# Split weights that begin 16 bytes lower with each turn through their three slots, and normalised x 32 bytes lower

## The chip, the core and the metric

The kernel runs on one core of one Trainium2 chip. The metric is the device time of one execution in microseconds. The core has five engines that run side by side: TensorE (PE in the profile, with PEld for its weight loads), VectorE (DVE), ScalarE (ACT), GpSimd (POOL) and SyncE (SP), which here issues DMAs. SBUF is the on-chip memory of 128 partitions; PSUM is where matmuls put their sums.

## The reference

One layer of a hybrid decoder on 512 tokens and 16 meta tokens (528 columns, called L), width 2048, all in float32:

```python
n = _rmsnorm(h, g_mix)                      # h: (528, 2048)
q, k, v, gb, gc, u = split(n @ w_in)        # six groups of 1024 columns
q, k = _rmsnorm(q, g_q), _rmsnorm(k, g_k)   # per head, 8 heads x 128
o_attn = stick_breaking_attention(q, k, v)  # strictly causal, cumulative log weights
o_conv = gb * causal_dwconv3(gc * u)
h = h + concat(_rmsnorm(o_attn), _rmsnorm(o_conv)) @ w_out
n2 = _rmsnorm(h, g_ffn)
h = h + (silu(n2 @ w_gate) * (n2 @ w_up)) @ w_down   # d_ff = 5632
```

## The kernel before

All activations are held transposed, channels on partitions and tokens along the row. To keep float32 accuracy with the fast float32r matmul, every weight and every activation is split into a high and a low part, and each 128x128 piece of a product is three matmuls: high weights by high activations, and the two mixed products. Every matmul has a weight load of its own, 128 columns of 4 bytes in each partition. The activations are the moving operand, 256, 258, 272 or 512 columns of 4 bytes.

**The split weights.** A piece is eight 128x128 tiles of raw weights, loaded by DMA into `sw_in`. `split_quad` (L197) splits it into `sw_split`: ACT copies the high part (L204), DVE subtracts to get the low part (L207). `sw_split` holds three slots of 8192 bytes in each partition, 4096 of high and 4096 of low parts. Pieces take the slots in turn, so a turn is three pieces, and the splits run two pieces ahead of PE (`S_AHEAD`, L153). The first ten pieces, which take part in the start of the program, lie in the same space as six halves of a slot, by another rule (L202). `prepare` (L236) says which piece is next, and `next_w` (L301) hands PE the oldest one. The order of all instructions follows from the program's own order, priorities and a tile scheduler.

**The normalised x.** Sixteen tiles `n_tiles` (L380) hold the high and the low part of x scaled by the norm's gain, each part a row of 528 columns. The tile has 160 bytes of free room ahead of what is used, and the low part stands 2304 bytes (nine times 256) behind the high part. A tile is 4608 bytes, eighteen times 256, so all sixteen begin at the same place modulo 256.

**Where they begin.** `pad_h` and `pad_n` are unused tiles that shift what is allocated around them. In the program as built, `sw_split` begins at byte 202624 of each partition, 128 modulo 256, and tile `n0` is used from byte 104256, 64 modulo 256. Slots, tiles within a slot, and the two parts are multiples of 512 bytes apart, so every weight load of split weights begins at 128 modulo 256. A matmul on `n` begins at 64 plus four bytes for each column that it skips.

**Who reads the normalised x.** `product_steps` (L327) makes the products of the heads: for each head k and v (each 256 and 272 columns, lines L337 and L339, tiles pk and pv) and q (512 columns from token 16 on, so 64 bytes further, tile pq). For each piece it runs 24 matmuls of one column part and then 24 of the other. Between them stand the small matmuls of the attention of the head before. After the eight heads come the first conv channels (`cu_product` L721, pc and pu, 258 columns, 56 bytes in; pb, 512 columns). Then `pair_product` (L861) makes the rest of the convolution in seven products for each pair of tiles, by a Strassen-like scheme, with `block_product` (L832, lines L848, L851, L852, 24 matmuls each). Four of the seven read `n` directly (`raw_block` L789, `last_block` L796), three read mixed sums of x kept in tiles `mixed`. `conv_pair` reads 258 columns, `gate_pair` 256 columns 8 bytes further. `last_block` begins 1032 bytes further on, which is 8 modulo 256.

**What does not read it.** The output projection reads tiles oa and oc, the FFN reads tiles f (and later ring and first); both take their weights from `sw_split`. The tiles f, ring and first are used from 240 modulo 256, the tiles mixed step by 8 bytes from tile to tile, and oa and oc are at 128.

Of the kernel before, what the change touches and what calls it, by code (L numbers as in the profile page):

```python
# [9 lines left out]
F32 = mybir.dt.float32  # L10
F32R = mybir.dt.float32r
# [4 lines left out]
P = 128  # L16
# [17 lines left out]
def hybrid_layer(ctx: ExitStack, tc: tile.TileContext, xT, w_in, w_out, w_gu, w_down, vecs, out):  # L34
# [12 lines left out]
    def open_pool(name, bufs=1, **kw):  # L47
        return tc.alloc_tile_pool(name=name, bufs=bufs, reuse_waits="tile", **kw)
# [3 lines left out]
    sw = open_pool("sw", side="right")  # L52
    npool = open_pool("npool", side="right")
# [50 lines left out]
    acc_h = hpool.tile([P, SEQ], F32, name="acc_h")  # L104
    hpool.tile([P, 24], F32, name="pad_h")
    sw_in = sw.tile([P, 6 * 8 * P], F32, name="sw_in")
    sw_split = sw.tile([P, 6 * 8 * P], F32R, name="sw_split")

    def w_place(t, n, i):
        return t[:, i * n * P : (i + 1) * n * P]  # L110
# [41 lines left out]
    quads, sums, split_w, used, wide, raws = {}, {}, [], [0], {}, []  # L152
    S_AHEAD = 2  # L153
# [42 lines left out]

    def split_quad(src, n, half=None, later=False):  # L197
        if half is None:
            at = (len(split_w) + 1) % (S_AHEAD + 1) * 16 * P
            hi, lo = (sw_split[:, at + i * n * P : at + (i + 1) * n * P] for i in range(2))  # L200
        else:
            at = half * 8 * P  # L202
            hi, lo = (sw_split[:, at + i * 4 * P : at + (i * 4 + n) * P] for i in range(2))
        sc.copy(hi, src)  # L204

        def low():
            latest[0] = ve.tensor_tensor(lo, src, hi.bitcast(F32), ALU.subtract)  # L207

        if not later:
            low()  # L210
        split_w.append((hi, lo))
        return low
# [23 lines left out]
    def prepare():  # L236
        kind, i, s = pieces[len(split_w)]
        with tc.high_priority():
            if kind == "first":
                at = len(split_w)  # L240
                split_quad(raws[at], s - i, at % 6)
                if at + 1 == n_first:
                    for i in (2, 3):
                        tc.keep_in_program_order(load_wide(0, i))
                return
            if kind == "wide":
                split_quad(wide[i, s], 8)
                load_wide(i, s + 4)
                return
# [4 lines left out]
            if s == 0:  # L254
                if i - 1 in (0, CONV):
                    low = split_quad(b["11"], n, later=True)

                    def rest():
                        low()
                        if i - 1 == CONV:  # L260
                            add_quads(i, "t1", b["11"], b["12"])
                        load_next(i, "11")

                    put_off.append(rest)
                    if i - 1 != CONV:
                        add_quads(i, "t1", b["11"], b["12"])
                    return
# [111 lines left out]
    H = L // 2  # L379
    n_tiles = [npool.tile([P, 2, L + 48], F32R, name=f"n{k}")[:, :, 40:] for k in range(KT)]  # L380
    n_parts = [[t[:, part] for part in range(2)] for t in n_tiles]
    npool.tile([P, 52], F32, name="pad_n")
    n_hl = []
    accs = [rpool.tile([P, L], F32, name=f"acc_x{i}") for i in range(2)]

# [103 lines left out]
    for t, row in zip(hosts, ((("kh", 384), ("kl", 384), ("sh", L), ("sl", L)), (("qh", SEQ), ("ql", SEQ), ("bh", 288), ("bl", 288)))):  # L489
        at = 0  # L490
# [659 lines left out]
    at = [(c, k) for c, n in enumerate(CHUNKS) for k in range(n)]  # L1150
# [199 lines left out]
```

## Time and profile before

| | |
|---|---|
| Runs | median of three 2032.04 us, from 2031.81 to 2034.05 |
| Profiled execution | 2031.66 us, of which 2029.9 us lie between the first and the last instruction |
| PE busy | 2021.6 us, clock granted in full throughout |
| DVE, ACT, POOL busy | 1725.7, 1080.3, 338.7 us |
| PE matmuls on `n` | 448.64 us of busy time, all before 600 us |
| Start to 30 us | first ten pieces, k and q of head 0 |
| 30 to 336 us | v of head 0, heads 1 to 7 |
| 336 to 387 us | first conv channels |
| 387 to about 600 us | conv in pairs |
| 600 to 2030 us | output projection, FFN |

A matmul row's duration in the profile runs from its issue to the end of its pipeline, longer than its share of PE: starts of successive matmuls are closer together than their durations are long. The spacing of starts is what a matmul costs in a stream, and is read from the timeline, from the first start of a stretch to the first start behind it, divided by the matmuls between. "x2" in a timeline row is two matmuls merged into one row.

### The profile page before, as it was taken

How to read it: one execution, taken by the hardware profiler on the slowest of the kernel's cores; microseconds unless marked ns; L12 is line 12 of the kernel's file. 1: busy time of each engine (PE TensorE's matmuls, PEld its weight loads, DVE VectorE, ACT ScalarE, POOL GpSimd, SP SyncE). 2: the span in 40 equal slices, each digit the busy share in tenths (PEclk: the TensorE clock that was granted, in tenths of full speed). 3: DMA queues.
4: the chain of work that ended last, by engine and by line, in shares of the span. 5: the costliest groups of instructions: out<-in, count | busy, mean ns of one | idle time of the engine just before them, and what ended most of it. 6: DMA issues, size and time to landing. Idle time of an engine off the chain costs nothing.

```text
span 2029.9 us, 39684 instructions
## 1 busy us (share of the span) xinstructions
PE 2021.6 (100%) x16158; PEld 1962.7 (97%) x16158; DVE 1725.7 (85%) x2196; ACT 1080.3 (53%) x1556; POOL 338.7 (17%) x507
## 2 busy tenths in 40 slices
PE   9999999999999999999999999999999999999999
PEld 8999999999998889999999999999999999999999
DVE  7877777698887778999998998998988978888888
ACT  7776666444454445555555555555555554444443
POOL 0111111200014440111110110110110243131211
PEclk9999999999999999999999999999999999999999
DMA  6343343823355555557555555555555999797864
GB/s 221 100 141 125 118 143 128 286 99 114 98 204 174 169 160 193 165 153 192 158 165 157 156 167 156 155 168 157 155 167 157 284 342 352 171 315 196 221 150 91
DMA packets 156231, 356.30 MB, mean 176 GB/s; under 512 B 13648, under 2 KB 67920, under 8 KB 155280
## 3 DMA queue, kind: packets, MB, share of 16 engines
q1 hardware_dynamic: 72352, 216.76, 33.4%
q0 software_dynamic: 83696, 136.99, 25.3%
q8 instruction: 127, 2.08, 0.4%
q14 instruction: 56, 0.46, 0.1%
HBM read 275.78 MB, written 77.92 MB: 174 GB/s over the span
## 4 chain that ended last, share of the span: by engine, by line
PE 50%; DVE 0%; issue 0%
PE x L848 10%; PE x L851 10%; PE x L852 10%; PE z L851 5%; PE z L848 5%; PE z L852 5%; PE y L851 2%; PE y L848 2%; PE y L852 2%; DVE d L1248 0%; DVE d L1250 0%
## 5 line engine op out<-in xcount | busy, mean ns | idle before, releaser
L204 ACT CAST sw_split<-sw_in 128x1024 fp32r<-128x1024 f32 (+2 forms) x668 | 662.9, 994 | 706.7 <-PE x L851 177.7
L207 DVE TENSOR_TENSOR sw_split<-sw_in,sw_split 128x1024 fp32r<-128x1024 f32 (+2 forms) x668 | 776.9, 1164 | 140.1 <-ACT sw_split L204 135.0
L848 PE MATMUL x<-f,sw_split 128*128 128x256 f32 x1408 | 387.6, 275 | 1.0 <-ACT sides L873 0.8
L852 PE MATMUL x<-f,sw_split 128*128 128x256 f32 x1408 | 387.4, 275 | 0.9 <-DVE sw_split L207 0.9
L851 PE MATMUL x<-f,sw_split 128*128 128x256 f32 x1408 | 387.3, 275 | 0.0
L848 PEld LDWEIGHTS x<-f,sw_split 128*128 128x128 f32 x1408 | 264.3, 188 | 1.7 <-ACT sides L873 1.2
L852 PEld LDWEIGHTS x<-f,sw_split 128*128 128x128 f32 x1408 | 264.3, 188 | 1.1 <-DVE sw_split L207 1.1
L851 PEld LDWEIGHTS x<-f,sw_split 128*128 128x128 f32 x1408 | 264.3, 188 | 0.0
L1159 POOL DMA_DIRECT2D fd<-s x147 | 103.9, 920 | 708.7 <-DVE s L350 633.2
L217 DVE TENSOR_TENSOR sw_in<-sw_in 128x1024 f32<-128x1024 f32 (+1 forms) x164 | 187.8, 1146 | 6.9 <-DMA sw_in<-w_in 1.5
L848 PE MATMUL z<-f,sw_split 128*128 128x256 f32 x704 | 193.6, 275 | 0.0
L851 PE MATMUL z<-f,sw_split 128*128 128x256 f32 x704 | 193.6, 275 | 0.0
L852 PE MATMUL z<-f,sw_split 128*128 128x256 f32 x704 | 193.6, 275 | 0.0
L848 PE MATMUL x<-ring,sw_split 128*128 128x256 f32 x608 | 167.2, 275 | 0.0
L851 PE MATMUL x<-ring,sw_split 128*128 128x256 f32 x608 | 167.2, 275 | 0.0
L852 PE MATMUL x<-ring,sw_split 128*128 128x256 f32 x608 | 167.2, 275 | 0.0
L852 PEld LDWEIGHTS z<-f,sw_split 128*128 128x128 f32 x704 | 132.2, 188 | 0.0
L851 PEld LDWEIGHTS z<-f,sw_split 128*128 128x128 f32 x704 | 132.2, 188 | 0.0
L848 PEld LDWEIGHTS z<-f,sw_split 128*128 128x128 f32 x704 | 132.1, 188 | 0.0
L848 PEld LDWEIGHTS x<-ring,sw_split 128*128 128x128 f32 x608 | 114.1, 188 | 0.0
L852 PEld LDWEIGHTS x<-ring,sw_split 128*128 128x128 f32 x608 | 114.1, 188 | 0.0
L851 PEld LDWEIGHTS x<-ring,sw_split 128*128 128x128 f32 x608 | 114.1, 188 | 0.0
(691 smaller groups left out, 5283.3 us busy)
## 6 DMA issues: line engine op xcount, KB each, us to landing
sw_in<-w_gu SPq DMA_DIRECT2D x176, 512.0 KB, 4.1
sw_in<-w_in SPq DMA_DIRECT2D x92, 512.0 KB, 3.4
fd<-s POOLq DMA_DIRECT2D x147, 256.0 KB, 5.2
sw_in<-w_down SPq DMA_DIRECT2D x96, 384.0 KB, 4.3
ring<-fd POOLq DMA_DIRECT2D x42, 768.0 KB, 17.5
sw_in<-w_out SPq DMA_DIRECT2D x32, 512.0 KB, 3.5
out_T<-d POOLq DMA_DIRECT2D x54, 256.0 KB, 4.8
mix_dram<-st_x POOLq DMA_DIRECT2D x16, 516.0 KB, 4.1
```

The source lines that it names most:

```text
L204: sc.copy(hi, src)
L207: latest[0] = ve.tensor_tensor(lo, src, hi.bitcast(F32), ALU.subtract)
L217: return ve.tensor_tensor(sums[name], a, b, ALU.add)
L848: opening = pe.matmul(p, hi[:, kk], ah, start=start and j == k == 0, stop=False, skip_group_check=skip)
L851: pe.matmul(p, hi[:, kk], al, start=False, stop=False, skip_group_check=skip)
L852: pe.matmul(p, lo[:, kk], ah, start=False, stop=k == n - 1, skip_group_check=skip)
L1159: gp.dma_start(fd[c][s][:, :, k], t[:, :, i])
```

## The change

Two things are edited, and one follows from them. `sw_split` gets 64 more columns (256 bytes). During the heads a piece no longer begins at its slot's beginning but up to 240 bytes behind it: `turn` counts the turns through the three slots, and the piece begins `max(18 - turn, 0) * 4` columns, so 16 bytes for each turn still to come, behind the slot's beginning. The first piece that goes this way is in turn 3 (240 bytes), the last piece of head 7 in turn 18 (0 bytes). All later pieces lie at the slot's beginning as before. The unused tile `pad_n` is dropped.

```diff
-    sw_split = sw.tile([P, 6 * 8 * P], F32R, name="sw_split")
+    sw_split = sw.tile([P, 6 * 8 * P + 64], F32R, name="sw_split")
...
     def split_quad(src, n, half=None, later=False):
         if half is None:
-            at = (len(split_w) + 1) % (S_AHEAD + 1) * 16 * P
+            turn, at = divmod(len(split_w) + 1, S_AHEAD + 1)
+            at = at * 16 * P + max(18 - turn, 0) * 4
             hi, lo = (sw_split[:, at + i * n * P : at + (i + 1) * n * P] for i in range(2))
         else:
             at = half * 8 * P
...
     n_tiles = [npool.tile([P, 2, L + 48], F32R, name=f"n{k}")[:, :, 40:] for k in range(KT)]
     n_parts = [[t[:, part] for part in range(2)] for t in n_tiles]
-    npool.tile([P, 52], F32, name="pad_n")
```

The pools on that side are allocated downwards. `sw_split` now begins 256 bytes lower (still 128 modulo 256), and with `pad_n` gone (224 bytes with its rounding) the tiles `n` begin 32 bytes lower, at 32 modulo 256. Where the operands begin, modulo 256, and the weights' begin minus that of x, here called the relation:

| stream | x before | weights before | relation before | x after | weights after | relation after |
|---|---|---|---|---|---|---|
| k, v (256, 272 columns) | 64 | 128 | 64 | 32 | 112, then each 16 lower, to 128 | every multiple of 16 |
| q (512) | 128 | 128 | 0 | 96 | the same | sweeps too |
| pc, pu, raw blocks (258) | 120 | 128 | 8 | 88 | 128 | 40 |
| last block (258) | 128 | 128 | 0 | 96 | 128 | 32 |
| raw blocks of gates (256) | 128 | 128 | 0 | 96 | 128 | 32 |
| last block of gates (256) | 136 | 128 | 248 | 104 | 128 | 24 |
| pb0, pb1 (512) | 128 | 128 | 0 | 96 | 128 | 32 |
| f, ring, first (256, FFN) | 240 | 128 | 144 | 240 | 128 | 144 |

Over the heads, k and v get 72 matmuls of each column count at each multiple of 32, and 24 at each odd multiple of 16. The relation stays the same through a piece and its 48 matmuls.

The order of the instructions is the same on every engine, and so are the waits, except two: the high part of the piece with index 10 waits for one more subtraction on DVE, and the low part of the piece with index 11 for a later matmul (PE's count 133 instead of 118), since the shifted pieces reach 224 to 240 bytes into the neighbouring half that one of the first ten pieces used.

## The prediction

> **What bounds the kernel now.** I read the page's first and fourth parts, then the stages, then single starts on the timeline.
>
> ```profile
> span 2029.9 us, 39684 instructions
> PE 2021.6 (100%) x16158; PEld 1962.7 (97%) x16158; DVE 1725.7 (85%) x2196; ACT 1080.3 (53%) x1556; POOL 338.7 (17%) x507
> PE 50%; DVE 0%; issue 0%
> PE warm L84 <- DVE one L80: 1.1, 1, 1.1
> ```
>
> PE is busy for the whole span, the chain that ended last names nothing else of weight, and PE's longest wait is 1.1 us. So the time is the sum of the spacings of matmuls, and only what changes a spacing counts. The change moves no instruction; it moves the places in SBUF that matmuls on `n` and their weight loads read. Busy time of PE on tile n, by stage:
>
> ```profile
> 0.00:30.00 30.00, 23.65 (x142) 1.00 0.85 304
> 30.00:336.00 306.00, 260.81 (x1774) 1.00 0.38 121
> 336.00:387.00 51.00, 45.58 (x293) 1.00 0.71 240
> 387.00:520.00 133.00, 74.53 (x606) 1.00 0.41 131
> 520.00:600.00 80.00, 44.07 (x360) 1.00 0.49 164
> ```
>
> Some 450 us are exposed; behind 600 us nothing reads n, and begins modulo 256 stay. Does the place matter at all? First starts, from the timeline (start, duration, engine, line):
>
> ```profile
> 1499.74 0.28 PE L852 MATMUL x<-f,sw_split 128*128 128x256 f32 x1
> 1503.03 0.28 PE L851 MATMUL z<-f,sw_split 128*128 128x256 f32 x1
> ...
> 178.91 0.28 PE L337 MATMUL pk<-n,sw_split 128*128 128x256 f32 x1
> 181.74 0.29 PE L337 MATMUL pk<-n,sw_split 128*128 128x272 f32 x1
> 184.70 0.39 PE L337 MATMUL pq<-n,sw_split 128*128 128x512 f32 x1
> 186.74 0.39 PE L337 MATMUL pq<-n,sw_split 128*128 128x512 f32 x1
> 188.08 0.40 PE L337 MATMUL pq<-n,sw_split 128*128 128x512 f32 x1
> 190.16 0.39 PE L337 MATMUL pq<-n,sw_split 128*128 128x512 f32 x1
> ...
> 440.82 0.28 PE L848 MATMUL x<-n,sw_split 128*128 128x258 f32 x1
> 443.71 0.28 PE L848 MATMUL y<-n,sw_split 128*128 128x258 f32 x1
> 446.57 0.28 PE L848 MATMUL x<-n,sw_split 128*128 128x258 f32 x1
> ...
> 460.81 0.28 PE L848 MATMUL x<-n,sw_split 128*128 128x256 f32 x1
> 463.85 0.28 PE L848 MATMUL y<-n,sw_split 128*128 128x256 f32 x1
> 466.72 0.28 PE L848 MATMUL x<-n,sw_split 128*128 128x256 f32 x1
> ```
>
> It does. With 256 columns and the same work:
> - f (relation 144): 3.29 us for 29 matmuls, 113.4 ns each
> - k (relation 64): 181.74 - 178.91 = 2.83 us for 24, 117.9 ns
> - gate block (relation 0): 466.72 - 463.85 = 2.87 us for 24, 119.6 ns
> - gate's last block (relation 248): 463.85 - 460.81 = 3.04 us for 24, 126.7 ns
>
> So a matmul costs up to 13.3 ns more than at the best place. My reading, which these rows suggest but don't prove, is that the stream of x and the load of the next matmul's weights, which run together, sometimes want the same part of SBUF, and the relation sets how often. Part of it is a matter of state: the 512-column q at relation 0 runs at 2.04 us for 9, 226.7 ns, and after the attention's small matmuls at 2.08 us for 9, 231.1 ns. Relation 64 knows two states too, here in head 1:
>
> ```profile
> 44.29 0.39 PE L339 MATMUL pk<-n,sw_split 128*128 128x256 f32 x2
> 45.31 0.39 PE L339 MATMUL pk<-n,sw_split 128*128 128x256 f32 x2
> ```
>
> 1.02 us for 9 is 113.3 ns, the best spacing, at a place that mostly gives 117.9.
>
> The Trainium skill, TensorE: Matmul & The Clock Gate, Part 2, step 1, says that PE has two independent SBUF read ports, one for the moving operand and one for weight loads, so that loading the next weights takes nothing from the running matmul. By that rule places do nothing and the sum is zero. The rows above disagree, 113.4 against 126.7 ns, and the measurement decides.
>
> **What is over the floor today.** From 256 columns at 113.4 to 512 at 226.7 ns a column costs 0.443 ns, so I take as floors (estimates) 114.3 ns for 258 columns and 120.5 for 272. Above them, by count of matmuls:
> - k and v, 256 columns: 4.5 ns x 720 = 3.2 us
> - k and v, 272 columns: (184.70 - 181.74) / 24 = 123.3 ns, so 2.8 x 720 = 2.0 us
> - q: between 0 and 4.4, about 2.2 x 336 = 0.7 us
> - 258 columns at relation 8: 2.86 / 24 = 119.2 ns, so 4.9 x 696 = 3.4 us
> - 258 columns at relation 0: 2.89 / 24 = 120.4 ns, so 6.1 x 168 = 1.0 us
> - gates: 6.2 x 216 + 13.3 x 72 = 2.3 us
> - pb: at the floor by the 226.7 of q, 96 matmuls
>
> Together 12.6 us is the most that better places could give back.
>
> **The change, part by part.** In the heads the relation sweeps all 16 multiples of 16, so the new price is a mean over them. No row shows such a sweep with one relation held for 48 matmuls. Bounds are 0 (f) and 13.3 ns (gate's last block). The nearest rows are the mixed tiles, which step through all places in steps of 8 bytes, three blocks of 24 each:
>
> ```profile
> 432.18 0.28 PE L848 MATMUL z<-mixed,sw_split 128*128 128x258 f32 x1
> 440.82 0.28 PE L848 MATMUL x<-n,sw_split 128*128 128x258 f32 x1
> ...
> 452.31 0.28 PE L848 MATMUL z<-mixed,sw_split 128*128 128x256 f32 x1
> 460.81 0.28 PE L848 MATMUL x<-n,sw_split 128*128 128x256 f32 x1
> ```
>
> 8.50 us for 72 is 118.1 ns, 4.7 over the floor with 256 columns; 8.64 for 72 is 120.0, 5.7 over with 258. The relations held at multiples of 16 (144, 64, 0) cost 0, 4.5 and 6.2, mean 3.6. Between 3.6 and 4.7 I take 4.2 ns for every stream of the heads:
> - 256 columns: (4.2 - 4.5) x 720 = -0.2 us
> - 272 columns: (4.2 - 2.8) x 720 = +1.0 us
> - q: (4.2 - 2.2) x 336 = +0.7 us
>
> After the heads each stream gets one new relation between 24 and 40, of which no row has a held price. Bounds are again 0 and 13.3. For 258 columns I take 5.5, between the held 4.9 and 6.1 and near the mixed 5.7: 0.6 x 696 - 0.6 x 168 = +0.3 us. For the gates the mixed 4.7: -1.5 x 216 - 8.6 x 72 = -0.9 us. For pb 4.2: +0.4 us.
>
> The start of the program (142 matmuls on n before 30 us, which wait for x) I cost at nothing, within 0.5 us either way.
>
> The splits, with 44 pieces at shifted places, I cost at nothing. Their engines have room in the heads, and pieces are two ahead:
>
> ```profile
> 30.00:336.00 306.00, 305.37 (x2099) 285.29 (x2098) 234.24 (x401) 217.18 (x361) 41.49 (x112) 1.00 0.38 121
> L204 ACT CAST sw_split<-sw_in 128x1024 fp32r<-128x1024 f32 (+2 forms) x668 | 662.9, 994 | 706.7 <-PE x L851 177.7
> 33.38 2.36 DVE L207 TENSOR_TENSOR sw_split<-sw_in,sw_split 128x1024 fp32r<-128x1024 f32 x2 [1.04 <-ACT sw_split L204]
> 24.08 1.06 ACT L204 CAST sw_split<-sw_in 128x1024 fp32r<-128x1024 f32 x1 [0.61 <-DMA sw_in<-w_in]
> 30.52 0.28 PE L337 MATMUL pv<-n,sw_split 128*128 128x256 f32 x1
> 36.31 0.28 PE L337 MATMUL pv<-n,sw_split 128*128 128x256 f32 x1
> ```
>
> The columns behind the length are busy time of PE, PEld, DVE, ACT, POOL: DVE idles 72 us of 306, ACT 89. Were the 44 copies of 994 ns twice as long, their 44 us would still fit, though DVE's subtractions wait behind them. Of the two new waits, that of piece 10's high part has the copy at 24.08 us, 5.4 us ahead of the first reader at 30.52; queued behind it on ACT is the read of pk, and a subtraction more is 1.2 us at most. That of piece 11's low part holds DVE, where the subtractions of pieces 11 and 12 stand at 33.38 us. The matmuls it must now await lie before pv's first at 30.52, so the wait ends 2.9 us ahead, and the piece is read from 36.31. No cost; were that cover gone, PE would be late by what passes 36.31. Further down, FFN and output projection keep their relations: zero.
>
> Sum: -0.2 + 1.0 + 0.7 + 0.3 - 0.9 + 0.4 = +1.3 us. The profiled execution took 2031.66 us, 0.4 under the median of the runs, and gives 2033.0.
>
> **Rivals.** *Slower, by bad places.* Relation 248 cost 13.3 ns. If 5 of the 16 relations of the sweep cost that and the others 4.2, the heads' mean is 7.0, and the heads give 2.5 x 720 + 4.2 x 720 + 4.8 x 336 = 6.4 us: 2038. It is over 0.2% from a mean of 5.8 ns on. For it speaks that 0 and 248 are both dear, so a dear stretch may be wide; against it that 248 came with x off the 16-byte grid, and every begin stays on it in the heads.
>
> *Faster, by locking.* The best spacing appears at relation 144 always and at 64 at times. If half of the heads' relations lie at the floor, mean 1.8, the heads give -2.7 x 720 - 1.0 x 720 - 0.4 x 336 = -2.8 us; if the relations 24 to 40 are at half of today's price as well, 6.7 / 2 = 3.4 us more: 2025.5. For it speaks head 1; against it that the mixed tiles, which pass every place, never come near the floor on average.
>
> *Nothing at all.* Were the places without effect, as the rule above has it, 2031.7. The rows leave it little.
>
> **How the numbers follow.** A measurement of this kernel tells about 0.2%, 4.1 us, from no change. The averaging case 0.55, bad places 0.27, locking 0.15, nothing 0.03; of the averaging case and its neighbours a few hundredths cross the bound either way. The time is the averaging case's 2033.0. Prices of 2 to 7 ns in the heads move it by about -4 to +5 us, and the relations after the heads at 2 or 8 ns by -4 to +3; the range 2027.5 to 2039 holds both rivals but their ends, the averaging case alone 2029 to 2036. Faster 0.15, the same 0.57, slower 0.28.
>
> **What would show it.** In the changed profile, k and v of different heads must differ in length, where now all heads are alike, with the spacing of 256 columns between 113 and 127 ns head by head; the gates' last block must fall from 126.7; f must stay at 113.4. The waits of PE must stay near 1 us in all. I am wrong if the heads' spacings hardly move (then the relation is not what matters), if the mean over the sweep lies below 2 or above 7 ns, or if PE waits for splits.

## The result, and the profile after

| | before | after |
|---|---|---|
| Median of 18 runs each | 2031.65 us | 2034.65 us |
| Ratio | | 1.0014, interval 1.0007 to 1.0020 |
| Profiled execution, span | 2029.9 us | 2032.7 us |
| PE busy | 2021.6 us | 2024.4 us |

The change costs about 3 us, 0.14%, inside the bound of 0.2%. The span and PE's busy time both grow by 2.8 us. First the page of the changed kernel (span, busy time by engine) and its longest PE wait:

```profile
span 2032.7 us, 39684 instructions
PE 2024.4 (100%) x16158; PEld 1964.2 (97%) x16158; DVE 1725.6 (85%) x2196; ACT 1078.9 (53%) x1556; POOL 338.9 (17%) x507
PE 50%; DVE 0%; issue 0%
PE warm L84 <- DVE one L80: 1.1, 1, 1.1
```

No wait was added: the longest is the 1.1 us of before. So the loss is in the matmuls. Busy time of PE on tile n in the changed kernel, by the same stages as in the prediction:

```profile
0.00:30.00 30.00, 23.54 (x142) 1.00 0.84 304
30.00:336.00 306.00, 260.90 (x1751) 1.00 0.38 121
336.00:387.00 51.00, 45.60 (x300) 1.00 0.65 219
387.00:520.00 133.00, 77.75 (x620) 1.00 0.44 136
520.00:600.00 80.00, 43.68 (x360) 1.00 0.50 168
sum 600.00, PE 451.47; mean PE 90.29
```

The sum is 451.47 us against 448.64, so the matmuls on n account for 2.83 us, all of the loss. Between 30 and 336 us the same busy time holds 1751 matmuls instead of 1774: the heads are slower, and some twenty matmuls slide into later stages (one that crosses a border counts in both). First starts in the changed kernel's timeline (start, duration, engine, line; lines between the edits are one further down):

```profile
129.24 0.28 PE L338 MATMUL pk<-n,sw_split 128*128 128x256 f32 x1
132.12 0.29 PE L338 MATMUL pk<-n,sw_split 128*128 128x272 f32 x1
...
179.73 0.28 PE L338 MATMUL pk<-n,sw_split 128*128 128x256 f32 x1
182.53 0.28 PE L338 MATMUL pk<-n,sw_split 128*128 128x272 f32 x1
...
74.96 0.29 PE L338 MATMUL pv<-n,sw_split 128*128 128x272 f32 x1
78.00 0.28 PE L338 MATMUL pv<-n,sw_split 128*128 128x256 f32 x1
...
285.65 0.29 PE L338 MATMUL pv<-n,sw_split 128*128 128x272 f32 x1
288.62 0.28 PE L338 MATMUL pv<-n,sw_split 128*128 128x256 f32 x1
...
269.66 0.40 PE L338 MATMUL pq<-n,sw_split 128*128 128x512 f32 x1
271.75 0.39 PE L338 MATMUL pq<-n,sw_split 128*128 128x512 f32 x1
...
464.16 0.28 PE L848 MATMUL x<-n,sw_split 128*128 128x256 f32 x1
467.04 0.28 PE L848 MATMUL y<-n,sw_split 128*128 128x256 f32 x1
469.89 0.28 PE L848 MATMUL x<-n,sw_split 128*128 128x256 f32 x1
...
1501.75 0.28 PE L851 MATMUL x<-f,sw_split 128*128 128x256 f32 x1
1503.11 0.28 PE L851 MATMUL x<-f,sw_split 128*128 128x256 f32 x1
```

Heads now differ, as the prediction asked. Blocks of 24:
- k of head 3 at relation 0: 2.88 / 24 = 120.0 ns; k of head 4 at relation 224: 2.80 / 24 = 116.7 (before: 117.7 to 117.9 in all heads, but for two blocks of head 1 at 113.3 to 113.5)
- 272 columns, v of head 1 at relation 48: 126.7 ns; v of head 6 at relation 144: 123.8 (before: 123.3)
- q of head 6 at relation 80: 2.09 / 9 = 232.2 ns (before: 226.7 to 231.1)
- the gates' last block: 120.0 (before 126.7); the gate block behind it 118.8 (before 119.6)
- f: 1.36 / 12 = 113.3, unchanged

Worked out from all starts of both traces, the 2.8 us split up like this (sums of spacings by product):

| part | change, us |
|---|---|
| heads 1 to 7: k, q, v | +0.85, +0.84, +1.04 |
| head 0, start of the program included | -0.2 |
| pc, pu | +0.2 |
| pb0, pb1 | +0.6 |
| conv in pairs | -0.6 |
| output projection | +0.2 |
| attention, FFN | -0.1 |

### The profile page after: what moved, and what is told of

It is laid out like the page before. It is cut to its first block, busy times and chain, and to the rows that moved or that the text cites. A ratio compares the mean times of both kernels' runs of the same rounds, so it can differ in the third digit from the quotient of the medians.

```text
span 2032.7 us, 39684 instructions
## 1 busy us (share of the span) xinstructions
PE 2024.4 (100%) x16158; PEld 1964.2 (97%) x16158; DVE 1725.6 (85%) x2196; ACT 1078.9 (53%) x1556; POOL 338.9 (17%) x507
## 4 chain that ended last, share of the span: by engine, by line
PE 50%; DVE 0%; issue 0%
PE x L848 10%; PE x L851 10%; PE x L852 10%; PE z L848 5%; PE z L851 5%; PE z L852 5%; PE y L848 2%; PE y L851 2%; PE y L852 2%; DVE d L1248 0%; DVE d L1250 0%
```

## The experiments

Three theories stood. A: the relation (weights' begin minus x's begin, modulo 256) sets the spacing. B: x's own begin does. C: neither, but the strides of the tiles or what ran just before. The diffs of the single parts stand against the kernel before, those further down against the changed kernel; those of the tables show their loops alone.

### A table of spacings

The layer is left out. Blocks of 24 matmuls (eight tiles, three matmuls each, each with its own weight load, as in the heads) run back to back for 16 begins of x times 16 begins of weights, with 256 and then with 272 columns.

```diff
+    for n in (256, 272):
+        for x_at in range(0, 256, 16):
+            for w_at in range(0, 256, 16):
+                block(n, x_at, w_at, 1152, 576)
```

> The layer is left out; only matmuls are timed, in groups of 24 that stream x past split weights with the strides of the heads. x begins at each of the 16 multiples of 16 modulo 256, the weights too, 256 groups with 256 columns and 256 with 272. Theory A (the relation, weights' begin minus x's begin, sets the spacing): the table is constant along its diagonals, 113.4 ns with 256 columns at relation 144, 118 at 64, 120 at 0. Theory B (the begin of x alone sets it): constant for each begin of x, lowest at 240. Theory C (neither; the state in which a stream falls, and the strides between the two parts of x): no pattern along rows, columns or diagonals, and a spread of a few ns.

Four neighbouring block starts with x at 32 (weights at 80, 96, 112 and the next), then two blocks with x at 48 (weights at 112 and 160), from the timeline:

```profile
124.52 0.28 PE L68 MATMUL bank<-both 128*128 128x256 f32 x1
127.34 0.28 PE L68 MATMUL bank<-both 128*128 128x256 f32 x1
130.07 0.28 PE L68 MATMUL bank<-both 128*128 128x256 f32 x1
132.92 0.28 PE L68 MATMUL bank<-both 128*128 128x256 f32 x1
...
175.53 0.28 PE L68 MATMUL bank<-both 128*128 128x256 f32 x1
178.25 0.29 PE L68 MATMUL bank<-both 128*128 128x256 f32 x1
...
183.94 0.28 PE L68 MATMUL bank<-both 128*128 128x256 f32 x1
186.67 0.28 PE L68 MATMUL bank<-both 128*128 128x256 f32 x1
```

With x at 32: 2.82 us at relation 48, 2.73 at relation 64, 2.85 at relation 80. Of these three only relation 64 is at the low spacing (113.3 ns in the middle of the block). With x at 48 relation 64 gives 2.72 us and relation 112 gives 2.73: both are low. The table is nearly constant along its diagonals, but there are two such patterns, one for x at 0 modulo 32 and one for x at 16 modulo 32. So theory A holds with a second condition. Exceptions remain: at relation 112 with x at 16 modulo 32, six of the eight begins of x give 113.3 ns and two give 118.8; on the other diagonals of 256 columns the eight differ by 2.5 ns at most. By medians of a diagonal, 256 columns cost 113.3 to 120.4 ns and 272 columns 123.2 to 126.7.

### One part of the change alone

x at 32 alone, weights as before:

```diff
-    npool.tile([P, 52], F32, name="pad_n")
```

> The kernel before with x at 32 instead of 64, weights not shifted (relation 96 for k and v, 32 for q, 40 and 32 and 24 behind the heads). Theory A: the heads take whatever relation 96 costs, alike in all heads, anywhere from 2 us less to 3 us more than before; behind the heads the same as the whole change, 0.3 us less. Theory B (x's own begin): the whole loss is here, 2.8 us more, and the shift adds nothing.

The sweep of the weights alone, x at 64. Everything else is kept in place by a wider `sw_split` and other pads, which the cut leaves out. Where the shift goes around from 0 to 60 columns, the first 60 columns of two pieces are overwritten before they are read, and four columns of an early piece too, so these products are not the layer's; PE still runs all its 16158 matmuls:

```diff
...
-            at = (len(split_w) + 1) % (S_AHEAD + 1) * 16 * P
+            turn, at = divmod(len(split_w) + 1, S_AHEAD + 1)
+            at = at * 16 * P + (max(18 - turn, 0) * 4 + 56) % 64
...
```

> The weights shifted 16 bytes lower with each turn through all 16 places during the heads, with x left at 64 (to make room the weights lie 32 bytes higher and every later piece is shifted back to 128; at one turn in head 6 the shift wraps around, which moves some 60 instructions there). Theory A: a sweep costs its mean over all relations whichever place x has, so the heads lose 2 to 3 us as in the whole change; behind the heads nothing changes. Theory B: x at 64 is as before, no change within 0.5 us.

x at 240 alone, so relation 144, where f runs:

```diff
-    n_tiles = [npool.tile([P, 2, L + 48], F32R, name=f"n{k}")[:, :, 40:] for k in range(KT)]
+    n_tiles = [npool.tile([P, 2, L + 48], F32R, name=f"n{k}")[:, :, 28:] for k in range(KT)]
...
-    npool.tile([P, 52], F32, name="pad_n")
```

> The kernel before with x at 240, as the activations of the FFN have it, weights at 128 (relation 144 for k and v). Theories A and B: k and v run at the FFN's spacing, 113.4 ns with 256 columns and 120.5 with 272, 5 us less in the heads. Theory C: the FFN's spacing comes from something else than these two begins, and the heads stay within 1 us of before.

| kernel | median, us | ratio to before, interval | 256 columns, ns | 272 | q, 512 and pb |
|---|---|---|---|---|---|
| before | 2031.6 | | 117.5 | 123.6 | 228.7 |
| changed | 2034.65 | 1.0014 (1.0007 to 1.0020) | 118.2 | 125.6 | 232.0 |
| x at 32 alone | 2033.69 | 1.0009 (1.0000 to 1.0018) | 117.6 | 123.8 | 233.2 |
| sweep alone | 2035.99 | 1.0019 (1.0010 to 1.0028) | 118.4 | 125.4 | 230.5 |
| x at 240 alone | 2033.03 | 1.0006 (0.9998 to 1.0015) | 115.9 | 125.1 | 232.8 |

(The last three columns are mean spacings in the stages up to pb, over all neighbouring matmuls of one width on n, without the few that are half as long again or more. The changed kernel's time and ratio are those of the result, against its own 2031.65.) With x at 32 alone, relation 96, k and v stay where they were, and q at relation 32 pays. Two starts of q six matmuls apart, from its timeline:

```profile
269.20 0.40 PE L337 MATMUL pq<-n,sw_split 128*128 128x512 f32 x1
270.60 0.40 PE L337 MATMUL pq<-n,sw_split 128*128 128x512 f32 x1
```

1.40 / 6 = 233.3 ns. The sweep alone makes k and v dear just as the whole change does. Busy time on n up to 600 us (448.64 before, 451.47 changed), with x at 32 alone and with the sweep alone:

```profile
0.00:600.00 600.00, 450.55 (x3168) 1.00 0.45 148
```

```profile
0.00:600.00 600.00, 451.68 (x3168) 1.00 0.45 148
```

The sweep's time is higher still, and its trace shows a wait on PE that the others do not have:

```profile
PE va L581 <- DVE tmp L574: 1.3, 1, 1.3
```

If these 1.3 us are taken off, it stands near the changed kernel. So the two edits do not add: by busy time on n, x at 32 alone costs 1.9 us, the sweep alone 3.0, and both together 2.8. The sweep takes the heads to about the mean of all relations, whatever x it starts from, and x at 32 then changes only what lies behind the heads, where gains and losses nearly cancel. x at 240 missed its expectation: 5 us less were expected, and it came out 1.4 us slower, which its interval does not tell from no change. Its 256 columns fell short of f's 113.4: 115.9 ns at the same relation and class, 1.2 us less by the sum of spacings. 272 columns gave 1.1 us back, and q and pb, at relation 80, cost 1.7 us more. That 256 columns stayed above 113.4 spoke for a part of theory C, a spacing that also depends on what ran before.

### The same relation at another place

x at 32 as changed, weights at 96 in the heads; their last piece and the first ten stay at 128:

```diff
-            at = at * 16 * P + max(18 - turn, 0) * 4
+            at = at * 16 * P + (56 if turn < 18 else 0)
```

> x at 32 as in the changed kernel, and the weights moved down by the same 32 bytes, to 96, for all turns of the heads: the relation is 64 for k and v and 0 for q, as before; behind the heads everything is as in the changed kernel. Theory A (the relation, with x modulo 32 as second condition, sets the spacing): the heads cost what they cost before (256 columns 117.6 ns, 272 columns 123.6, q 228.7), behind the heads as with x alone at 32 (pb +0.6 us, 258 columns +0.2, gates -0.6): +0.2 us in all, 2031.9. Theory B (x's or the weights' own begin sets it): the heads are dear as in the changed kernel or with x alone at 32, q at 233 ns and more, +1.4 us or more.

Measured: 2031.60 us against 2031.66, ratio 1.0001 (0.9992 to 1.0010). Busy time on n up to 600 us in this kernel (451.47 changed, 448.64 before):

```profile
0.00:600.00 600.00, 448.57 (x3168) 1.00 0.45 148
```

And q of head 6 in this kernel, six matmuls apart:

```profile
268.22 0.39 PE L338 MATMUL pq<-n,sw_split 128*128 128x512 f32 x1
269.58 0.39 PE L338 MATMUL pq<-n,sw_split 128*128 128x512 f32 x1
```

1.36 / 6 = 226.7 ns, back from 233. Both operands stand 32 bytes lower and the heads cost what they did before. Theory B is out, and the loss of the heads is undone by the relation alone, while the shifted slots and the missing pad stay. What changed behind the heads (pb +0.6, pairs -0.6) nearly cancels.

### The same relation in the other class

x at 48 and weights at 112: relations as before, x at 16 modulo 32.

```diff
-            at = at * 16 * P + max(18 - turn, 0) * 4
+            at = at * 16 * P + (60 if turn < 18 else 0)
...
-    n_tiles = [npool.tile([P, 2, L + 48], F32R, name=f"n{k}")[:, :, 40:] for k in range(KT)]
+    n_tiles = [npool.tile([P, 2, L + 48], F32R, name=f"n{k}")[:, :, 44:] for k in range(KT)]
```

> x at 48 and the weights at 112 during the heads: the relations as before (64, and 0 for q), but x's begin is now 16 modulo 32. Theory A: where this class of x, which has more low places, holds the low spacing better, 256 columns fall from 117.6 ns to between 113.3 and 116, 720 matmuls x 1.6 to 4.3 ns = 1.2 to 3.1 us less in the heads, 272 columns 123.3 to 125.2, so 2029 to 2032 in all. If the class does nothing: heads as before, 2031 to 2032.5. Theory C (what ran just before decides, not the place): 256 columns 117.6 ns again.

Measured: 2030.71 us, ratio 0.9996 (0.9987 to 1.0005). k of head 4:

```profile
169.90 0.28 PE L338 MATMUL pk<-n,sw_split 128*128 128x256 f32 x1
172.62 0.28 PE L338 MATMUL pk<-n,sw_split 128*128 128x272 f32 x1
```

2.72 / 24 = 113.3 ns, where the kernel before has 117.9 at the same relation. The mean over the heads is 114.7. So the class of x matters in the kernel too. Busy time on n falls by 1.7 us, but the measured time is not told from no change by its interval; q rises to 231.1 ns in this class.

### Tables with other widths and strides, and with other blocks ahead

The layer is left out in both. The first has 512 columns, 258 columns (x in steps of 8), and 256 columns with the strides of f; the second, whose loop follows, runs at each pair of places 256, 272, 256 and 512 columns in turn, weights' places falling.

```diff
+    for x_at in range(0, 256, 16):
+        for w_at in reversed(range(0, 256, 16)):
+            block(256, x_at, w_at, 1152, 576)
+            block(272, x_at, w_at, 1152, 576)
+            block(256, x_at, w_at, 1152, 576)
+            block(512, x_at, w_at, 1152, 576)
```

> The layer is left out (the output is not the layer's): three tables of spacings, 512 columns and 258 columns with the strides of n, 256 columns with the strides of f. Theory A: constant along the diagonals in the two classes of x; 512 columns with few low relations at 226.7 ns and the rest 229 to 233, with relation 0 low or in both states, and 32 near 233; 258 columns low at relation 64 near 114.2 and 119 to 121 elsewhere; with f's strides 113.3 at relation 144 for x at 16 modulo 32, as in the table with n's strides. Theory C (strides or state decide): the table with f's strides looks different from that with n's.

> The layer is left out (the output is not the layer's): at each pair of places 24 matmuls with 256 columns, 24 with 272, 24 with 256, 24 with 512, and the weights' places in falling order. Theory A: both groups of 256 show the table of before, 113.3 ns at the same places. Theory C (what ran just before decides as well): the second group of 256, which follows 272 columns, is above 113.3 at some places where the table shows 113.3, as the heads of the kernel before are (117.6 at relation 64).

With f's strides the table of 256 columns is the one of n's strides, place by place to 0.1 ns: relation 144 with x at 16 modulo 32 gives 113.3 again, which is what f shows. So these strides, all multiples of 256 bytes, do nothing. For 258 columns the expected low at relation 64 did not come: 121.0 and 120.0 ns in the two classes, two columns away from 113.3. What ran just before does something. Block starts of the second kernel with x at 32, weights at 96 (256, 272, 256, 512 columns), then with x at 48, weights at 112:

```profile
604.07 0.28 PE L68 MATMUL bank<-both 128*128 128x256 f32 x1
606.90 0.29 PE L68 MATMUL bank<-both 128*128 128x272 f32 x1
609.87 0.28 PE L68 MATMUL bank<-both 128*128 128x256 f32 x1
612.69 0.40 PE L68 MATMUL bank<-both 128*128 128x512 f32 x1
...
817.45 0.28 PE L68 MATMUL bank<-both 128*128 128x256 f32 x1
820.20 0.28 PE L68 MATMUL bank<-both 128*128 128x272 f32 x1
823.16 0.28 PE L68 MATMUL bank<-both 128*128 128x256 f32 x1
825.88 0.39 PE L68 MATMUL bank<-both 128*128 128x512 f32 x1
```

At relation 64 and x at 32 the blocks of 256 columns take 2.83 and 2.82 us, where the block among its like took 2.73. At x 48 they take 2.75 and 2.72: in that class the low spacing of relation 64 survives a block of another width. That is the 117.5 of the kernel before against the 114.7 of x at 48. It does not survive everywhere in that class: at relation 112 both blocks of 256 columns go from 113.3 to 118.7 ns. And it goes the other way too. Four block starts with x at 80 and weights at 16, relation 192, which costs 118.3 ns among its like:

```profile
1358.60 0.28 PE L68 MATMUL bank<-both 128*128 128x256 f32 x1
1361.33 0.28 PE L68 MATMUL bank<-both 128*128 128x272 f32 x1
1364.34 0.28 PE L68 MATMUL bank<-both 128*128 128x256 f32 x1
1367.17 0.40 PE L68 MATMUL bank<-both 128*128 128x512 f32 x1
```

Behind the 512 columns of the place before, the first block takes 2.73 us, 113.3 ns a matmul in its middle; behind 272 columns the third takes 2.83. The table below has medians over the eight begins of x in each class, in ns. "Alone" is the first table; the other columns are the mixed one, where "256" is the mean of the two blocks (so 115.8 at relation 192 stands for 113.3 and 118.3).

| relation | x 0 mod 32: 256 alone | 256 | 272 | 512 | x 16 mod 32: 256 alone | 256 | 272 | 512 |
|---|---|---|---|---|---|---|---|---|
| 0 | 119.7 | 119.8 | 125.3 | 227.2 | 118.3 | 118.2 | 125.3 | 231.1 |
| 16 | 118.5 | 118.3 | 125.1 | 233.4 | 117.3 | 117.1 | 125.0 | 236.7 |
| 32 | 118.5 | 118.3 | 125.3 | 233.3 | 120.0 | 119.8 | 125.4 | 226.7 |
| 48 | 117.8 | 117.8 | 124.7 | 233.3 | 119.5 | 119.0 | 126.3 | 234.7 |
| 64 | 113.3 | 117.8 | 123.4 | 233.3 | 113.3 | 113.6 | 123.3 | 228.8 |
| 80 | 118.9 | 118.7 | 127.1 | 232.0 | 119.4 | 119.4 | 123.3 | 233.2 |
| 96 | 117.3 | 117.3 | 123.3 | 234.4 | 117.8 | 116.7 | 123.3 | 226.7 |
| 112 | 120.4 | 119.9 | 126.8 | 233.1 | 113.3 | 118.7 | 124.4 | 233.1 |
| 128 | 120.2 | 118.7 | 126.5 | 232.4 | 120.0 | 119.9 | 126.8 | 233.3 |
| 144 | 118.3 | 120.0 | 123.3 | 233.3 | 113.3 | 115.6 | 123.7 | 230.8 |
| 160 | 119.9 | 120.1 | 125.3 | 233.1 | 119.9 | 119.9 | 125.5 | 233.3 |
| 176 | 118.0 | 118.0 | 125.6 | 230.0 | 120.0 | 118.4 | 125.0 | 230.9 |
| 192 | 117.8 | 117.9 | 126.7 | 228.9 | 118.3 | 115.8 | 125.2 | 226.7 |
| 208 | 116.7 | 116.7 | 125.8 | 231.8 | 118.3 | 118.4 | 125.0 | 233.3 |
| 224 | 116.7 | 116.7 | 126.0 | 233.3 | 118.3 | 118.3 | 126.7 | 233.3 |
| 240 | 120.0 | 118.7 | 125.0 | 226.7 | 116.7 | 117.7 | 124.5 | 231.7 |

The mixed columns priced over the relations that a kernel's heads really have, from v of head 0 on, give these means, beside what its trace shows:

| heads of | 256: table, trace | 272: table, trace | q: table, trace |
|---|---|---|---|
| before | 117.8, 117.5 | 123.4, 123.6 | 227.2, 229.2 |
| changed | 118.4, 118.2 | 125.4, 125.6 | 231.5, 231.5 |
| x at 32 alone | 117.3, 117.6 | 123.3, 123.8 | 233.3, 233.2 |
| x at 240 alone | 115.6, 115.9 | 123.7, 125.1 | 233.2, 232.6 |
| x at 48, weights at 112 | 113.8, 114.7 | 123.4, 123.7 | 231.1, 231.1 |

A table without the layer thus gives the changed kernel's heads to within 0.3 ns, and x at 240's 256 columns, which the table of blocks alone puts at 113.3. Two gaps remain. 272 columns with x at 240 cost 1.4 ns more than the table, unexplained. And q of before is at the table's 226.7 to 227.2 part of the time and near 231 behind the attention's small matmuls, which no table contains.

### Places chosen from the tables

x at 80 and k's and v's weights at 144 (relation 64, x at 16 modulo 32), q's weights at 80 (relation 192), all but those of the first ten pieces; and in a second kernel also the weights at 112 for what lies between the heads and the output projection (relation 232 for most 258-column products, where the table shows 115.8 ns). To find the room, `pad_h` and the last tile of n are smaller, so the low part of that one tile stands elsewhere modulo 256.

```diff
-    hpool.tile([P, 24], F32, name="pad_h")
+    hpool.tile([P, 16], F32, name="pad_h")
...
-    sw_split = sw.tile([P, 6 * 8 * P + 64], F32R, name="sw_split")
+    sw_split = sw.tile([P, 6 * 8 * P + 72], F32R, name="sw_split")
...
-            at = at * 16 * P + max(18 - turn, 0) * 4
+            if turn < 18 or (turn == 18 and at == 0):
+                at = at * 16 * P + ((52 if at < 2 else 68) if turn % 2 else (68 if at else 4))
+            else:
+                at = at * 16 * P + (60 if turn < 44 else 0)
...
-    n_tiles = [npool.tile([P, 2, L + 48], F32R, name=f"n{k}")[:, :, 40:] for k in range(KT)]
+    n_tiles = [npool.tile([P, 2, L + (48 if k < KT - 1 else 22)], F32R, name=f"n{k}")[:, :, 4:] for k in range(KT)]
```

(The first of the two kernels has 0 in place of `60 if turn < 44 else 0`.)

> Places chosen from the tables, in the heads alone: x at 80 (16 modulo 32), weights of k and v at 144 (relation 64), those of q at 80 (relation 192, where the tables with and without another block ahead both give 226.7 ns at 512 columns). Theory A, with the tables as prices: 256 columns 113.3 to 114.7 ns, 272 columns 123.3 to 123.7, q 226.7 to 228: against the kernel before -3 us in the heads, about 2028.8 in all, with the pairs within 0.5 us. If the tables do not carry over to the kernel: 2030 or more.

> As the kernel with chosen places in the heads, and behind the heads the weights at 112 until the output projection: the 678 matmuls with 258 columns on n at 136 then stand at relation 232, where the table shows 115.8 ns with x at 8 modulo 32. Theory A: 258 columns at that place fall from 119.5 to about 115.8, 678 x 3.7 ns = 2.5 us less, and 168 at x 144 rise by about 1 ns, so about 2026.5 in all. If a block on another tile ahead takes the low spacing away, as it did at relation 64 with 256 columns: 118 to 120 ns, and 2028.8 as without it.

| kernel | median, us | before beside it | ratio, interval | 256 | 272 | 258 in pc, pu / pairs |
|---|---|---|---|---|---|---|
| heads only | 2029.87 | 2031.44 | 0.9989 (0.9980 to 0.9998) | 114.5 | 124.2 | 119.0 / 118.4 |
| heads and conv | 2028.24 | 2031.44 | 0.9982 (0.9973 to 0.9991) | 114.5 | 124.2 | 116.2 / 117.1 |

Busy time on n of the first and of the second, by the same view, and two starts 24 matmuls apart in the second kernel's pairs:

```profile
0.00:600.00 600.00, 446.25 (x3168) 1.00 0.45 149
```

```profile
0.00:600.00 600.00, 444.13 (x3168) 1.00 0.45 149
```

```profile
386.23 0.28 PE L851 MATMUL y<-n,sw_split 128*128 128x258 f32 x1
389.02 0.28 PE L851 MATMUL x<-n,sw_split 128*128 128x258 f32 x1
```

2.79 / 24 = 116.3 ns for 258 columns, where the kernel before has 119.2 to 120.4. So the tables carry over, not in full: the heads gain 1.7 us by their spacings (3 expected), the conv stage 1.6 us in time (2.3 expected from 2028.8 to 2026.5). The heads' rest is 272 columns at 124.2 ns instead of 123.3, and q at 228.0. By sums of spacings the first kernel also gained 1.1 us behind the heads (pairs -1.5, pb +0.4), where at most 0.5 was expected, so its time alone does not show what the heads gave. Both kernels are faster than the kernel before and the second by 0.18%. The second one's profiled execution took 2031.77 us, the longest of its runs, and shows a wait for a transfer in the FFN:

```profile
PE x L854 <- DMA f<-fx: 1.9, 1, 1.9
```

Its FFN is therefore not compared.

## Why the prediction was right, and where not

The forecast was 2033.0 us, and its sum +1.3 us; measured are 2034.65 and +2.8 by span, +3.0 by the medians (ratio 1.0014). The measured time lies within the range and within 0.2%, as the likeliest outcome said, and PE's spacings alone carry the loss, as forecast: the relation sets them, with conditions that the prediction did not have. The sum itself was less than half of what came. That the stream of x and the weight load meet in the same part of SBUF, the reading behind it, is not shown: the runs vary where the two begin, and none takes the loads away. The terms:

| term | forecast, us | measured, us |
|---|---|---|
| heads, 256 columns (720) | -0.2 | 118.2 - 117.5 = 0.7 ns, +0.5 |
| heads, 272 columns (720) | +1.0 | 125.6 - 123.6 = 2.0 ns, +1.4 |
| q (336) | +0.7 | 231.5 - 229.2 = 2.3 ns, +0.8 |
| 258 columns | +0.3 | about +0.4 |
| gates (288) | -0.9 | 118.8 - 121.6 = -2.8 ns, -0.8 |
| pb (96) | +0.4 | +0.6 |
| start, splits, FFN | 0 | -0.2 at the start, +0.2 in the output projection |

The heads' products add up to 2.7 us by spacings, and to the same by their own sums, which also hold the borders to other matmuls. The forecast had 1.5 for them.

*The step that was mis-sized* is the price of the sweep, 4.2 ns over the floor for every stream. Over the prediction's own floors it measured 118.2 - 113.4 = 4.8 ns at 256 columns, 125.6 - 120.5 = 5.1 at 272 and 231.5 - 226.7 = 4.8 for q. For 272 columns the floor itself was wrong as well. It was drawn as a line between 256 and 512 columns, 120.5 ns; the tables show 123.3 as the lowest at any place, and 125.3 as the mean of the mixed column. So the kernel before stood at the floor with its 123.3, not 2.8 ns above it, and a sweep could only lose. Over the true floor the sweep cost 2.3 ns, so one price for every width does not hold either; that the term came within 0.4 us owes something to two errors of opposite sign. For 256 columns the mean over places with x at 0 modulo 32 is 118.2 to 118.4, not the 117.6 that 4.2 over 113.4 gives: the three held relations averaged included f, which is one of the few low places of the other class of x. The mixed tiles' 118.1 ns, the other row weighed in that step, was the better price. q did not sweep all 16 places: each head has its own, and heads 1 to 7 stand at the seven odd multiples of 16 from 48 to 240. The mixed table's mean over these is 231.5 ns, as the trace's.

*The reading of f was incomplete.* f's 113.4 was taken as the price of relation 144. It is the price of 144 with x at 16 modulo 32. In the changed kernel x is at 0 modulo 32 and the same relation gives 119.3.

*The two states of relation 64* were seen in head 1 and called a matter of state. The mixed table shows a part of what sets it: a block of another width ahead takes the low spacing away. It is not all. In the kernel before, one block of head 1's v runs at 113.5 ns right behind the attention's matmuls of tile c, and the blocks of v that follow the same matmuls in heads 2 to 7 run at 117.7. Two blocks of the changed kernel at the same relation come down to 113.3 as well. What sets that stays open.

*Nothing at all* is excluded. The Trainium skill, TensorE: Matmul & The Clock Gate, Part 2, step 1, gives moving operand and weight load read ports of their own, so that a load takes no read bandwidth from the running matmul. Here the same 24 matmuls with the same loads take 2.73 us at one begin and 2.85 sixteen bytes on; the measurement decides.

*Bad places* and *locking* did not come: no relation in the heads cost more than 120 ns at 256 columns, and in the changed kernel only two blocks came down to 113.3, both at relation 64 (the second of v in head 0, after its first matmuls, and the first of k in head 1). The 126.7 ns of the gates' last block belong to its relation of 248 with x at 8 modulo 32; at relation 24, in the same class of x, it fell to 120.0, where 118.1 was forecast.

*Splits and waits* cost nothing, as forecast: PE's longest wait is still 1.1 us. *FFN* stayed. The 0.2 us of the output projection, whose places did not move, stayed unexplained.

## What to carry to other kernels

Where PE is busy throughout and each matmul loads its own weights, the begin of the moving operand and that of the weights are worth a table: run the kernel's own mix of widths over both begins modulo 256, and choose from it. Vary one thing at a time, and measure each width by itself, since a floor drawn between two widths was 2.8 ns off here. Sweeping a place gives the mean of all places, which loses against a place that was already good.

## What was not expected of the hardware

- The pattern over the relation is not one but two, by x at 0 or 16 modulo 32: at 256 columns one low relation (64) in the one, three (64, 112, 144) in the other, all 113.3 ns by medians against 116.7 to 120.4 elsewhere. With x at 8 modulo 32 and 258 columns there is a low of 115.8 at relation 232. The strides of x tried, multiples of 256 bytes, did not matter.
- The spacing has a memory: at relation 64 and x at 0 modulo 32, 113.3 ns among blocks of the same width and 117.8 behind blocks of 272 or 512 columns. In the other class relation 64 keeps its 113.3, relation 112 rises to 118.7, and relation 192 falls from 118.3 to 113.3 behind 512 columns.
- 512 columns stand at 226.7 ns in few places and up to 236.7 in others, ten nanoseconds between begins 16 bytes apart. Why these places and not others remains open; the runs show the pattern, not the arrangement of the memory behind it.
